# Low, low, high, high: the order of a k-tile's four feature-major products

## The chip, the core and the metric

The kernel runs on one core of one Trainium2 chip. TensorE (PE in the profile) multiplies matrices, VectorE (DVE) and ScalarE (ACT) work element by element, GpSimd (POOL) and SyncE (SP) mostly issue transfers. The metric is the device time of one execution in microseconds (us), taken as the median of several runs.

## The reference

The reference is two transformer-like blocks, one behind the other, on 256 tokens of 2048 features, in float32. The first has two kinds of attention, a gated merge, a feed-forward network and an embedding gate; the second a state-space branch, a gated linear attention, a differential attention, and a feed-forward network with a convolution. Nearly all of the arithmetic is in products of an activation matrix and a large weight matrix, each weight read once:

```
proj = h @ w_in[i]                                   # 2048 x 10240
...
g_ff, u_ff = jnp.split(h @ w_ffn_in[i], 2, axis=-1)  # 2048 x 11264
x = x + (jax.nn.silu(g_ff) * u_ff) @ w_ffn_out[i]
...
proj = hn @ w_in[l]
...
u = h @ w_up                                         # 2048 x 11008
```

## The kernel before

All large products are jobs in one list, and `stream` runs them one after the other. A weight arrives in blocks of 128 x 1024 numbers (512 KB) that SyncE loads; such a block is called a half. To keep nearly all of float32's accuracy, a number is split in two: a high part, rounded to TensorE's one-pass format (`fp32r`), and a low part, the remainder. For weights, ACT makes the high part (line 487, `high`) and DVE the low part (line 497, `low`), a few halves ahead of their use: `CA` = 4 halves for the high part, `SA` = 3 for the low one. Both go to fixed places in one large tile `w`, so a new high or low part waits until TensorE has read the old one in its place. Activations lie as `x = j.acts.at(k)`: 128 features by 512 columns, 256 tokens' high parts and then the same tokens' low parts.

There are two main kinds of job. A token-major job (kind "AS", `mm_as`, lines 591 to 593) has the activations as stationary operand and 512 columns of weights moving; each of its products has 512 columns. A feature-major job (kind "WS", lines 549 to 559) has the weights as stationary operand and the tokens moving. It makes two blocks of 128 output features, f = 0 and f = 1, from 2048 input features, which are 16 k-tiles of 128; one half holds four k-tiles, so a job has four halves. For each k-tile and block there are two products:

- the high product (line 553): high weights times all 512 columns of `x`, into `acc[:, f, :]`
- the low product (line 557): low weights times the 256 high columns of `x`, into `acc[:, f, 256:512]`

The two blocks lie in separate accumulators of 512 numbers each. In the job's first k-tile the high product comes first, since it starts the accumulation (`start=k == first`); in all others the low one does. After the last k-tile the job's evacuation (`ws_sum`: ACT copies one part out at line 445, DVE adds the other at line 446) is put in front of the other waiting work, and the next job begins on the other of two accumulators. Before each new half, the loop issues the splitting of a later half, and after it `self.tick()` lets the rest of the program (attention, norms, evacuations) issue its next piece; small matmuls of that rest so come to stand between two halves. The instructions of each engine are run in the order in which this loop writes them.

Of the kernel before, what the change touches and what calls it, by code (L numbers as in the profile page):

```python
# [188 lines left out]
class Build:  # L189
# [262 lines left out]
    def stream(self, jobs):  # L452
        nc = self.nc
        halves = [(j, i, ks) for j in jobs for i, ks in j.halves]
        N = len(halves)
        raws, spl = {}, {}
        width = lambda j, ks: {"AS": 512 * len(ks), "WS": 1024, "W4": 512}[j.kind]

        W = self.wp.tile([128, (CA + 1) * 1024 + GAP + (SA + 1) * 1024 + WSH], F32R, tag="w", name="w")

        def places(first, bufs):


            far = [False] * (N + 1)
            for i in reversed(range(N)):
                far[i] = halves[i][0].kind == "WS" and (far[i + 1] or i % bufs == bufs - 1)
            at = [first + i % bufs * 1024 + WSH * far[i] for i in range(N)]
            return at, {i for i in range(bufs, N) if far[i] and i % bufs != bufs - 1 and not far[i - bufs + 1]}

        at_h, late_h = places(0, CA + 1)  # L470
        at_l, late_l = places((CA + 1) * 1024 + GAP, SA + 1)

        def load(i):
            j, idx, ks = halves[i]
            n = width(j, ks)
            r = self.rawp.tile([128, 1024], F32, tag="raw", name=self.name("raw"))
            nc.sync.dma_start(out=r[:, :n], in_=self.d[j.w][idx][:, :n])
            raws[i] = r

        def high(i):  # L480
            j, idx, ks = halves[i]
            n = width(j, ks)
            wh = W[:, at_h[i]:at_h[i] + 1024]
            if j.kind == "W4":
                wh = self.ev.tile([128, 512], F32, tag="b", name=self.name("w4"), bufs=1)
            for c in ((0, 512), (512, n)) if i == 0 else ((0, n),):
                nc.scalar.copy(wh[:, c[0]:c[1]], raws[i][:, c[0]:c[1]])  # L487
            spl[i] = wh

        def low(i):  # L490
            j, idx, ks = halves[i]
            n = width(j, ks)
            r, wh = raws.pop(i), spl[i]
            wl = None
            if j.kind != "W4":
                wl = W[:, at_l[i]:at_l[i] + 1024]
                nc.vector.tensor_sub(wl[:, :n], r[:, :n], wh[:, :n].bitcast(F32))  # L497
            spl[i] = (wh, wl)
            if i + RAWB < N:
                load(i + RAWB)  # L500

        ahead = self.at_start(load)

        z = self.ev.tile([128, 512], mybir.dt.bfloat16, tag="b", name="zeros", bufs=1)
        nc.vector.memset(z, 0.0)
        b = self.psp.tile([128, 512], F32, tag="p3", name="idle")
        for _ in range(WARM):
            nc.tensor.matmul(b, lhsT=z[:, 0:128], rhs=z, start=True, stop=True)
        for i in range(CA):
            next(ahead)  # L510
            high(i)
            if i < SA:
                low(i)
        self.add(ahead)
        last, prev, acc = None, None, None
        for i, (j, idx, ks) in enumerate(halves):
            if i + CA < N and i + CA not in late_h:
                high(i + CA)
            if i + SA < N and i + SA not in late_l:
                low(i + SA)  # L520
            if j is not last:
                if j.before is not None:
                    j.before()
                while prev is not None and not prev.free:
                    self.tick(must=True)
                prev, last = last, j
                acc = self.accp.tile([128, 2, 512], F32, tag="acc", name=self.name("acc"))
            for k in ks:
                while k not in j.acts.ready:
                    self.tick(must=True)  # L530
            first, end = j.halves[0][1][0], j.halves[-1][1][-1]
            if j.by_m is not None:

                for m in range(2):
                    for q, (_, _, kq) in enumerate(halves[i:]):
                        self.mm_as(j.acts, kq, *spl[i + q], acc, (m,), first, end)
                    j.by_m(m, acc)
                break
            wh, wl = spl.pop(i)
            if j.kind == "AS":  # L540
                self.mm_as(j.acts, ks, wh, wl, acc, (0, 1), first, end, low_last=i < 2)
            elif j.kind == "W4":

                for k in range(16):
                    p = slice(32 * (k % 4), 32 * (k % 4) + 32)
                    nc.tensor.matmul(acc[p, 0, :], lhsT=wh[:, 32 * k:32 * k + 32],
                                     rhs=j.acts.at(k).bitcast(F32), start=k < 4, stop=k >= 12)
            else:
                for kk, k in enumerate(ks):
                    x = j.acts.at(k)  # L550
                    for f in range(2):
                        s = slice((kk * 2 + f) * 128, (kk * 2 + f) * 128 + 128)
                        hi = lambda: nc.tensor.matmul(  # L553
                            acc[:, f, :], lhsT=wh[:, s], rhs=x, start=k == first, stop=k == end)
                        if k == first:
                            hi()
                        nc.tensor.matmul(acc[:, f, 256:512], lhsT=wl[:, s], rhs=x[:, 0:256], start=False, stop=False)  # L557
                        if k != first:
                            hi()
            if i + CA in late_h:  # L560
                high(i + CA)
            if i + SA in late_l:
                low(i + SA)
            if i + 1 == N or halves[i + 1][0] is not j:
                self.add(j.evac(acc, lambda j=j: setattr(j, "free", True)), front=True)
            self.tick()
        while self.gens:
            self.tick(must=True)
# [1238 lines left out]
```

## Time and profile before

| what | value |
|---|---|
| median of 3 runs | 3137.13 us (3136.98 to 3137.66) |
| the profiled execution, its time | 3137.06 us |
| the profiled execution, its span | 3135.3 us |
| PE busy | 3122.8 us, 17644 matmuls |
| DVE, ACT busy | 1993.8 us, 1551.2 us |
| high products of feature-major jobs (line 553) | 3936 |
| low products of feature-major jobs (line 557) | 3936 |
| token-major products (lines 591, 592, 593) | 2368 each |

The span goes from the first to the last instruction. Matmuls overlap in the records: one of 512 columns is listed with 393 ns, while the next one starts sooner, and their ends are modelled. So the rate is read from the distance of their starts. PEld is the load of a stationary operand; it too overlaps with matmuls.

### The profile page before, as it was taken

How to read it: one execution, taken by the hardware profiler on the slowest of the kernel's cores; microseconds unless marked ns; L12 is line 12 of the kernel's file. 1: busy time of each engine (PE TensorE's matmuls, PEld its weight loads, DVE VectorE, ACT ScalarE, POOL GpSimd, SP SyncE). 2: the span in 40 equal slices, each digit the busy share in tenths (PEclk: the TensorE clock that was granted, in tenths of full speed). 3: DMA queues.
4: the chain of work that ended last, by engine and by line, in shares of the span. 5: the costliest groups of instructions: out<-in, count | busy, mean ns of one | idle time of the engine just before them, and what ended most of it. 6: DMA issues, size and time to landing. Idle time of an engine off the chain costs nothing.

```text
span 3135.3 us, 45198 instructions
## 1 busy us (share of the span) xinstructions
PE 3122.8 (100%) x17644; PEld 2650.9 (85%) x17644; DVE 1993.8 (64%) x2595; ACT 1551.2 (49%) x2035; POOL 73.3 (2%) x158
## 2 busy tenths in 40 slices
PE   9999999999999999999999999999999999999998
PEld 7888888888888888888888888888888888888887
DVE  5656445557577676566655667945555766757766
ACT  6544444455444454456544455444445645545544
POOL 0000000000001000000000001000000000000000
PEclk9999999999999999999999999999999999999999
DMA  7554555555667667655654565655555565565554
GB/s 267 175 179 164 191 192 188 185 186 190 215 226 249 243 229 238 189 175 195 215 178 162 176 219 201 217 183 201 197 187 185 185 196 188 190 198 188 190 188 168
DMA packets 172646, 618.00 MB, mean 197 GB/s; under 512 B 23553, under 2 KB 23969, under 8 KB 169233
## 3 DMA queue, kind: packets, MB, share of 16 engines
q1 hardware_dynamic: 164704, 576.96, 55.9%
q0 software_dynamic: 7440, 37.64, 3.5%
q8 instruction: 138, 2.26, 0.3%
q14 instruction: 76, 0.61, 0.1%
q10 hardware_dynamic: 288, 0.52, 0.0%
HBM read 599.74 MB, written 14.25 MB: 196 GB/s over the span
## 4 chain that ended last, share of the span: by engine, by line
PE 99%; DMA 0%; DVE 0%; ACT 0%; SPq 0%; issue 0%; ACTq 0%
PE acc L553 29%; PE acc L591 17%; PE acc L592 17%; PE acc L593 17%; PE acc L557 15%; PE p L349 1%; PE p L1712 0%; PE p L1752 0%; DMA raw<-in_w_vsb 0%; PE p L1165 0%; PE p L939 0%; PE p L940 0%; PE p L941 0%; PE p L1161 0%; PE p L1755 0%; PE p L1142 0%
## 5 line engine op out<-in xcount | busy, mean ns | idle before, releaser
L497 DVE TENSOR_TENSOR w<-raw,w 128x1024 fp32r<-128x1024 f32 x1088 | 1319.4, 1219 | 642.3 <-PE acc L592 429.1
L487 ACT CAST w<-raw 128x1024 fp32r<-128x1024 f32 (+1 forms) x1089 | 1138.5, 1048 | 1091.8 <-PE acc L593 641.6
L553 PE MATMUL acc<-s,w 128*128 128x512 f32 x3936 | 1369.5, 393 | 0.0
L557 PE MATMUL acc<-s,w 128*128 128x256 f32 x3936 | 1090.4, 282 | 0.0
L591 PE MATMUL acc<-w,s 128*128 128x512 f32 x2368 | 930.5, 393 | 0.8 <-DVE big L1385 0.8
L592 PE MATMUL acc<-w,s 128*128 128x512 f32 x2368 | 922.1, 389 | 0.4 <-DVE w L497 0.4
L593 PE MATMUL acc<-w,s 128*128 128x512 f32 x2368 | 922.0, 389 | 0.0
L553 PEld LDWEIGHTS acc<-s,w 128*128 128x128 f32 x3936 | 733.5, 188 | 153.4
L557 PEld LDWEIGHTS acc<-s,w 128*128 128x128 f32 x3936 | 740.2, 188 | 10.4 <-issue 1.0
L593 PEld LDWEIGHTS acc<-w,s 128*128 128x128 f32 x2368 | 444.5, 188 | 93.6
L591 PEld LDWEIGHTS acc<-w,s 128*128 128x128 f32 x2368 | 444.6, 188 | 93.4 <-issue 1.7
L592 PEld LDWEIGHTS acc<-w,s 128*128 128x128 f32 x2368 | 444.7, 188 | 91.8 <-DVE w L497 1.3
L446 DVE TENSOR_TENSOR s<-acc,s 128x512 f32<-128x512 f32 (+1 forms) x120 | 82.7, 689 | 267.7 <-ACT s L445 267.6
L445 ACT COPY s<-acc 128x512 f32<-128x512 f32 (+1 forms) x120 | 70.1, 584 | 187.4 <-PE acc L553 185.0
L313 ACT ACTIVATE s<-s 128x256 f32<-128x256 f32 (+4 forms) x175 | 76.6, 443 | 106.9 <-DVE s L316 38.1
L316 DVE SCALAR_TENSOR_TENSOR s<-s,conv 128x256 f32<-128x256 f32 x172 | 79.3, 481 | 3.1
L448 DVE TENSOR_TENSOR s<-s,rb 128x512 f32<-128x512 f32 (+1 forms) x104 | 71.7, 689 | 3.5
L321 ACT CAST s<-s 128x256 fp32r<-128x256 f32 (+1 forms) x104 | 45.7, 443 | 29.4 <-DVE s L979 14.3
L1668 DVE TENSOR_TENSOR s<-s,s 128x1024 f32<-128x1024 f32 x48 | 58.4, 1218 | 0.0
L313 ACT ACTIVATE s<-s,conv 128x256 f32<-128x256 f32 x86 | 47.1, 595 | 21.9 <-DVE s L448 21.9
L322 DVE TENSOR_TENSOR s<-s,s 128x256 fp32r<-128x256 f32 (+1 forms) x104 | 47.3, 457 | 15.2 <-ACT s L321 13.9
L313 ACT ACTIVATE junk<-big 128x512 f32<-128x512 f32 x48 | 30.3, 631 | 51.2 <-DVE big L958 32.4
(268 smaller groups left out, 1015.3 us busy)
## 6 DMA issues: line engine op xcount, KB each, us to landing
raw<-in_w_fin SPq DMA_DIRECT2D x176, 512.0 KB, 4.3
raw<-in_w_up SPq DMA_DIRECT2D x172, 512.0 KB, 4.1
raw<-in_w_fout SPq DMA_DIRECT2D x88, 512.0 KB, 4.5
raw<-in_w_down SPq DMA_DIRECT2D x84, 512.0 KB, 4.2
raw<-in_w_qksb SPq DMA_DIRECT2D x32, 512.0 KB, 3.8
raw<-in_w_qkca SPq DMA_DIRECT2D x32, 512.0 KB, 4.2
raw<-in_w_gsb SPq DMA_DIRECT2D x32, 512.0 KB, 4.1
raw<-in_w_gca SPq DMA_DIRECT2D x32, 512.0 KB, 3.8
```

What stands on the lines that cost most here:

```text
L313: self.nc.scalar.activation(out, in_, func, scale=scale, **kw)
L316: self.nc.vector.scalar_tensor_tensor(out=out, in0=in0, scalar=scalar, in1=in1, op0=op0, op1=op1)
L445: nc.scalar.copy(out, acc[:, 0:n, 256:512])
L446: nc.vector.tensor_add(out, acc[:, 0:n, 0:256], out)
L448: nc.vector.tensor_mul(out, out, rb.tile[:, None, :].to_broadcast([128, n, 256]) if n > 1 else rb.tile[:, None, :])
L487: nc.scalar.copy(wh[:, c[0]:c[1]], raws[i][:, c[0]:c[1]])
L497: nc.vector.tensor_sub(wl[:, :n], r[:, :n], wh[:, :n].bitcast(F32))
L553: hi = lambda: nc.tensor.matmul(acc[:, f, :], lhsT=wh[:, s], rhs=x, start=k == first, stop=k == end)
L557: nc.tensor.matmul(acc[:, f, 256:512], lhsT=wl[:, s], rhs=x[:, 0:256], start=False, stop=False)
L591: nc.tensor.matmul(acc[:, m, :], lhsT=xl, rhs=wh[:, s], start=k == first, stop=False)
L592: nc.tensor.matmul(acc[:, m, :], lhsT=xh, rhs=wl[:, s], start=False, stop=False)
L593: nc.tensor.matmul(acc[:, m, :], lhsT=xh, rhs=wh[:, s], start=False, stop=k == end)
```

## The change

In every k-tile of a feature-major job the loop over high and low goes outside the loop over the two blocks. A k-tile other than a job's first ran low f0, high f0, low f1, high f1, and now runs low f0, low f1, high f0, high f1. The first one ran high f0, low f0, high f1, low f1, and now runs high f0, high f1, low f0, low f1. Operands, shapes, places and the order of the additions into each accumulator stay.

```diff
                     x = j.acts.at(k)
-                    for f in range(2):
-                        s = slice((kk * 2 + f) * 128, (kk * 2 + f) * 128 + 128)
-                        hi = lambda: nc.tensor.matmul(
-                            acc[:, f, :], lhsT=wh[:, s], rhs=x, start=k == first, stop=k == end)
-                        if k == first:
-                            hi()
-                        nc.tensor.matmul(acc[:, f, 256:512], lhsT=wl[:, s], rhs=x[:, 0:256], start=False, stop=False)
-                        if k != first:
-                            hi()
+                    for is_low in (False, True) if k == first else (True, False):
+                        for f in range(2):
+                            s = slice((kk * 2 + f) * 128, (kk * 2 + f) * 128 + 128)
+                            if is_low:
+                                nc.tensor.matmul(acc[:, f, 256:512], lhsT=wl[:, s], rhs=x[:, 0:256],
+                                                 start=False, stop=False)
+                            else:
+                                nc.tensor.matmul(acc[:, f, :], lhsT=wh[:, s], rhs=x, start=k == first, stop=k == end)
```

In the changed file the low product is line 555 and the high one line 558. The instructions of DVE, ACT, GpSimd and SyncE keep their order, number and kinds of waits. On TensorE, this is the start of one job, `acc122`, before (s is the tile of the activations, w the weights; like neighbours are one row with x2):

```order
L553 MATMUL acc122_1024<-s40_144,w_105 128x512 [waits PE_49]
L557 MATMUL acc122_1024<-s40_144,w_105 128x256
L553 MATMUL acc122_1024<-s40_144,w_105 128x512
L557 MATMUL acc122_1024<-s40_144,w_105 128x256 x2
L553 MATMUL acc122_1024<-s40_144,w_105 128x512
L557 MATMUL acc122_1024<-s40_144,w_105 128x256
L553 MATMUL acc122_1024<-s40_144,w_105 128x512
L557 MATMUL acc122_1024<-s40_144,w_105 128x256
L553 MATMUL acc122_1024<-s40_144,w_105 128x512
```

The first two highs stand apart, and the only two lows in a row are the last of the first k-tile and the first of the second. The same place on TensorE now:

```order
L558 MATMUL acc122_1024<-s40_144,w_105 128x512 [waits PE_49]
L558 MATMUL acc122_1024<-s40_144,w_105 128x512
L555 MATMUL acc122_1024<-s40_144,w_105 128x256 x4
L558 MATMUL acc122_1024<-s40_144,w_105 128x512 x2
L555 MATMUL acc122_1024<-s40_144,w_105 128x256 x2
L558 MATMUL acc122_1024<-s40_144,w_105 128x512 x2
```

The first k-tile's lows and the second's make a row of four, and from then on lows and highs come in twos. The second place is the seam of two halves of the same job, where small matmuls of an attention (p123) stand between; TensorE before:

```order
L553 MATMUL acc122_1024<-s40_144,w_105 128x512
L721 MATMUL p123_1045<-s119_1011 128x256 [waits DVE_49,PE_49]
L722 MATMUL p123_1045<-s119_1011 128x128
L557 MATMUL acc122_1024<-s43_164,w_105 128x256
L553 MATMUL acc122_1024<-s43_164,w_105 128x512 [waits Activation_49]
L557 MATMUL acc122_1024<-s43_164,w_105 128x256
```

The half's first high, which waits for ACT, is its second product. TensorE now:

```order
L558 MATMUL acc122_1024<-s40_144,w_105 128x512 x2
L720 MATMUL p123_1045<-s119_1011 128x256 [waits DVE_49,PE_49]
L721 MATMUL p123_1045<-s119_1011 128x128
L555 MATMUL acc122_1024<-s43_164,w_105 128x256 x2
L558 MATMUL acc122_1024<-s43_164,w_105 128x512 [waits Activation_49]
L558 MATMUL acc122_1024<-s43_164,w_105 128x512
```

It is now the third product, and the half before ends with two highs, so its last low is read one product earlier.

## Rows read from the trace of the kernel before

**Rows 1.** The page: busy time (share of the span), 40 slices in tenths.

```profile
span 3135.3 us, 45198 instructions
...
PE 3122.8 (100%) x17644; PEld 2650.9 (85%) x17644; DVE 1993.8 (64%) x2595; ACT 1551.2 (49%) x2035; POOL 73.3 (2%) x158
...
PEclk9999999999999999999999999999999999999999
```

**Rows 2.** The page: the chain that ended last, by engine and line.

```profile
PE 99%; DMA 0%; DVE 0%; ACT 0%; SPq 0%; issue 0%; ACTq 0%
...
by line: PE acc L553 28.8%; PE acc L591 17.2%; PE acc L592 17.1%; PE acc L593 17.1%; PE acc L557 14.9%; PE p L349 0.7%; PE p L1712 0.3%; PE p L1752 0.2%; DMA raw<-in_w_vsb 0.2%; PE p L1165 0.2%; PE p L939 0.2%; PE p L940 0.2%; PE p L941 0.2
```

**Rows 3.** PE's waits, all: total us, times, longest us.

```profile
PE idle L508 <- DVE zeros L505: 1.3, 1, 1.3
PE acc L583 <- ACT w L487: 0.8, 2, 0.6
PE acc L591 <- DVE big L1385: 0.8, 1, 0.8
PE acc L592 <- DVE w L497: 0.4, 1, 0.4
```

**Rows 4.** Timeline of PE in token-major work: start us, us, instruction.

```profile
350.12 0.39 PE L591 MATMUL acc<-w,s 128*128 128x512 f32 x1
...
371.88 0.39 PE L591 MATMUL acc<-w,s 128*128 128x512 f32 x1
```

**Rows 5.** Timeline of PE in the middle of a feature-major job.

```profile
2525.36 0.28 PE L557 MATMUL acc<-s,w 128*128 128x256 f32 x1
2525.47 0.39 PE L553 MATMUL acc<-s,w 128*128 128x512 f32 x1
2525.70 0.28 PE L557 MATMUL acc<-s,w 128*128 128x256 f32 x1
...
2533.68 0.28 PE L557 MATMUL acc<-s,w 128*128 128x256 f32 x1
```

**Rows 6.** Timeline of PE at seams of feature-major jobs, the last high first.

```profile
2434.12 0.62 PE L553 MATMUL acc<-s,w 128*128 128x512 f32 x2
...
2523.03 0.62 PE L553 MATMUL acc<-s,w 128*128 128x512 f32 x2
2523.49 0.28 PE L557 MATMUL acc<-s,w 128*128 128x256 f32 x1
2523.61 0.39 PE L553 MATMUL acc<-s,w 128*128 128x512 f32 x1
2523.84 0.40 PE L557 MATMUL acc<-s,w 128*128 128x256 f32 x2
2524.07 0.40 PE L553 MATMUL acc<-s,w 128*128 128x512 f32 x1
2524.31 0.28 PE L557 MATMUL acc<-s,w 128*128 128x256 f32 x1
...
2534.14 0.62 PE L553 MATMUL acc<-s,w 128*128 128x512 f32 x2
```

**Rows 7.** Groups of PE and PEld: count, busy us, mean ns, idle us before.

```profile
L553 PE MATMUL acc<-s,w 128*128 128x512 f32 x3936 | 1369.5, 393 | 0.0
L557 PE MATMUL acc<-s,w 128*128 128x256 f32 x3936 | 1090.4, 282 | 0.0
...
L557 PEld LDWEIGHTS acc<-s,w 128*128 128x128 f32 x3936 | 740.2, 188 | 10.4 <-issue 1.0
```

**Rows 8.** Timeline of PE: a feature-major job behind token-major work, up to its end.

```profile
2809.26 0.39 PE L593 MATMUL acc<-w,s 128*128 128x512 f32 x1
2809.49 0.39 PE L553 MATMUL acc<-s,w 128*128 128x512 f32 x1
...
2820.36 0.62 PE L553 MATMUL acc<-s,w 128*128 128x512 f32 x2
...
2821.16 0.40 PE L557 MATMUL acc<-s,w 128*128 128x256 f32 x2
2821.40 0.40 PE L553 MATMUL acc<-s,w 128*128 128x512 f32 x1
```

**Rows 9.** Waits of the engines that split the weights: total us, times, longest us.

```profile
ACT w L487 <- PE acc L553: 240.5, 187, 3.0
...
DVE w L497 <- PE acc L557: 78.6, 64, 3.8
```

## The prediction

> **What bounds the kernel now.** I read the page from the top. TensorE (PE) is busy for 3122.8 of 3135.3 us, its clock is granted in full (2.4 GHz, the upper of its two levels) in all 40 slices, and the other engines stand at 64% and below [rows 1]. A busy PE alone proves little, since matmuls overlap in the records, so the chain that ended last comes next: 99% of it is PE, and 28.8% and 14.9% of the span are lines 553 and 557, the two lines of the change [rows 2]. Then the list of PE's own waits: in the whole program they are 3.3 us, of which 0.4 us are for a low half of weights from VectorE (DVE) [rows 3]. So nothing feeds PE too late; the time is the rate at which PE starts one matmul after the other. I read that rate from the distances of starts in the timeline, over whole repetitions, since single starts are rounded to 10 ns and the ends are modelled.
>
> Three rates count. In a token-major job every matmul has 512 columns: 96 of them take from 350.12 to 371.88, 226.7 ns each [rows 4]. In the middle of a feature-major job a low (256 columns) and a high (512) alternate: 24 pairs take from 2525.36 to 2533.68, 346.7 ns a pair [rows 5]. If a high costs 226.7 here too, a low costs 120.0; the difference for 256 columns is then 106.7 ns, and twice that for 512 columns is 213.3, so that 13.3 ns remain for each matmul, long or short. Both steady stretches fit "columns plus 13.3 ns", whatever their mix. Last, whole jobs: nine jobs, each of 32 pairs, take from 2434.12 to 2534.14, 11.113 us a job [rows 6]. Thirty-two pairs at 346.7 ns are 11.093. Each job thus loses 0.020 us, and it loses it at the seam, because the middle runs at the steady rate.
>
> **The change, part by part.** The matmuls stay the same in number and shape: 3936 highs and 3936 lows [rows 7], four to a k-tile, so 1968 k-tiles in 123 jobs. The instructions of the other engines stand in the same order as before. What moves is the order inside a k-tile, and with it three things.
>
> *The rate.* In 1845 k-tiles (all but the first of each job) low, high, low, high becomes low, low, high, high. Each k-tile then has one low behind a low and one high behind a high. Before, both neighbourhoods occur at the seam of two jobs alone: the last high of a job stands before the first of the next, and the low that ends the first k-tile stands before the one that begins the second. Their rows: two highs from 2523.03 to 2523.49, 0.46 us, against 0.453 for two at 226.7 ns; two lows from 2523.84 to 2524.07, 0.23 us, against 0.240 [rows 6]. Together 0.69 us, against 0.693 for the k-tile of now. By its four matmuls the new k-tile costs what the old one does. What the seam loses comes just behind the two lows: from the second of them, which starts 0.12 us behind the first, at 2523.96, to the low at 2525.36 four pairs take 1.40 us, where the steady rate gives 1.387 [rows 5, 6]. That row decides the upper bound, because in the new order every two lows are followed not by steady pairs but by the next change of neighbourhood. If each k-tile loses all that a seam loses, 0.020 us, the change costs 1845 x 0.020 = 37 us. From below: the two lows at 0.23 us read up to 0.010 under 2 x 120 ns; since another pair of lows takes 0.24 (2821.16 to 2821.40 [rows 8]), I put it at 0.005 us, and if the highs behind give nothing of it back, that is 1845 x 0.005 = 9 us gained. Between the two ends, a job that follows token-major work has the two lows in its start, but no two highs across its seam: from its first high at 2809.49 to the next job's first high, which begins 0.23 us after the 2820.36 of its row, so at 2820.59, are 11.10 us [rows 8], 0.007 over 32 pairs, with a rounding of 0.010. So two lows alone cost some 5 ns at most, a quarter of the seam. I take 0: two steady stretches of quite different make-up, all long and long with short, both run at 13.3 ns over the columns, and the new order is again a steady repetition, where the seam's loss is that of a change from one pattern to another. Taken: 0 us; ends -9 and +37.
>
> *The seam.* Each job's first k-tile goes high, high, low, low, where it went high, low, high, low, so four highs and then four lows stand in a row. At worst the loss there doubles, at best it goes: 123 x 0.020 = 2.5 us either way; taken 0.
>
> *Due times and releases.* The last reader of a low half now comes one high before the half's end, 0.23 us earlier, so the copy that overwrites it (line 497) may start earlier in each of the 1968 / 4 = 492 halves. DVE waited for these lows 64 times, 78.6 us in all [rows 9]. But what it makes is waited for by PE for 0.4 us in the program [rows 3], so that this is worth 0.4 us at most. The first low of a job comes one high later, the first high of every other half one low (0.12 us) later: slack for DVE and for ScalarE (ACT). The last reader of a high half stays the second block's high, so ACT's 240.5 us of waits for line 553 [rows 9] stay, and so does the start of the evacuation. No DMA and no queue is moved past. Taken 0.
>
> The sum is made against the profiled execution, 3137.06 us, which is 3135.3 of span and 1.8 around it, and 0.07 under the median of the runs, 3137.13: 3137.1 + 0 + 0 + 0 = **3137.1 us**.
>
> A rule of the Trainium skill bears on the two lows: the page "TensorE: Matmul & The Clock Gate", section "LDWEIGHTS (loading the stationary operand)", gives a weight load as its columns over 1.2 GHz, by an estimate from it 107 ns for 128 columns. A low's 115 to 120 ns cover that by some 10 ns, and by the rule alone two lows in a row cost nothing: the sum stays as it is. The records of this kernel give 188 ns for a load [rows 7], more than the distance of two lows, and so speak for the first rival below; but one after another four of them would make 752 ns a k-tile, where 693 pass, so they overlap and set no price.
>
> **The rivals.**
> *Slower: the lows in a row eat a reserve.* PE prepares the next weights and products while the present one runs; behind a high there is twice the time for that as behind a low. If an alternating stream lives on what each high builds up for the low behind it, two lows in a row use it up, and the pairs behind them pay, as the four pairs behind 2523.96 do. For it: a loss at every seam of nine equal jobs, and of equal size. Against it: after token-major work the same two lows cost a quarter of that. It decides against the forecast from 6.3 / 1845 = 3.4 ns a k-tile. At the 5 ns of the start behind token-major work: 1845 x 0.005 = +9, **3146 us**; at the full seam +37, 3174.
> *Faster: lows in a row are cheaper.* If the 0.23 us of two lows holds and the highs run at 226.7, a k-tile takes 0.688 and the program 9 us less: **3128 us**. Against it: the pairs behind the two lows give it all back, and more [rows 6].
> *The change doesn't do what it says* in one sense: if PE's start of a matmul depends on columns alone, no order inside a k-tile shows in the time. That is the forecast itself.
>
> **How the numbers follow.** A measurement of this kernel can tell about 0.2%, 6.3 us, from no change. The forecast, no change that shows (3134.5 to 3143), gets 0.55. The slower rival gets 0.37, of which I put 0.22 under 3151 (a loss of up to 7.5 ns a k-tile: 1845 x 0.0075 = 14 us) and 0.15 above it. The faster one gets 0.08. The range holds the forecast's cases and the cheaper half of the slower ones, 0.77, and a little of the faster: 3134 to 3151. Most of the chance lies on no change and on slower; the forecast's own range is 3134.5 to 3143. So faster 0.08, same 0.55, slower 0.37.
>
> **What would show it.** In the timeline of the changed kernel, twelve k-tiles in the middle of a job should take 8.32 us, as 24 pairs do now, and a job 11.09 to 11.13. If the slower rival is right, the k-tile takes 0.697 us or more throughout the job, two highs behind two lows take over 0.46, and PE still waits for nothing. PE's waits should stay near 3 us, and DVE's for the lows shrink from 78.6. The forecast is wrong if a k-tile's period differs from 0.693 by more than 0.003, for I argue its rate from seams alone, and the trace of before has no steady stretch of the new order.

## The result, and the profile after

The changed kernel takes 3155.54 us (3155.34 to 3155.70 in 4 runs), where the kernel before takes 3137.06 (3136.98 to 3137.66 in 4 runs): 1.0058 times as long, 95% interval 1.0046 to 1.007. It is 18.5 us slower. The forecast, 3137.1 us and no change that shows, was wrong, and the range, 3134 to 3151, does not hold the time.

The page of the changed kernel, against [rows 1, 2]; the high product is now line 558, the low one line 555:

```profile
span 3153.9 us, 45198 instructions
...
PE 3141.6 (100%) x17644; PEld 2654.2 (84%) x17644; DVE 1993.1 (63%) x2595; ACT 1551.7 (49%) x2035; POOL 73.6 (2%) x158
...
PEclk9999999999999999999999999999999999999999
```

PE does the same 17644 matmuls and is busy 18.8 us longer; the clock is granted in full as before, and DVE and ACT are as busy as before. PE's waits, all of them (total us, times, longest us), against [rows 3]:

```profile
PE idle L508 <- DVE zeros L505: 1.3, 1, 1.3
PE acc L590 <- DVE big L1384: 0.8, 1, 0.8
PE acc L582 <- ACT w L487: 0.6, 1, 0.6
PE acc L591 <- DVE w L497: 0.4, 1, 0.4
```

They sum to 3.1 us, where they were 3.3: none has come in. The groups of the two lines (count, busy us, mean ns of one, idle us before), against [rows 7]:

```profile
L558 PE MATMUL acc<-s,w 128*128 128x512 f32 x3936 | 1229.0, 396 | 0.0
...
L555 PE MATMUL acc<-s,w 128*128 128x256 f32 x3936 | 772.7, 283 | 0.0
```

A high is recorded with 396 ns instead of 393, a low with 283 instead of 282. The busy sums of the two lines can't be compared with those of before, since time in which two matmuls overlap is put down to one of them. So the starts have to be read. PE in the middle of a feature-major job (start us, us, instruction; x2 is two alike in one row), against [rows 5]:

```profile
2661.92 0.40 PE L555 MATMUL acc<-s,w 128*128 128x256 f32 x2
2662.16 0.63 PE L558 MATMUL acc<-s,w 128*128 128x512 f32 x2
2662.63 0.40 PE L555 MATMUL acc<-s,w 128*128 128x256 f32 x2
...
2668.99 0.40 PE L555 MATMUL acc<-s,w 128*128 128x256 f32 x2
```

From 2661.92 to 2668.99 ten k-tiles take 7.07 us, 707 ns each, where two pairs of before take 2 x 346.7 = 693.3. Most of the loss sits in the highs. Two lows take 0.24 us (2661.92 to 2662.16) and two highs 0.47 (2662.16 to 2662.63), some 234 ns each. In the middle of a job of before, the next start comes 0.23 us behind a high and 0.11 behind a low [rows 5]; without the timeline's rounding to 10 ns, the trace of before gives 229 and 117.5 ns there, and that of the changed kernel 234 to 235 and 117 to 120. So some 10 of the 13.3 ns are the two highs'. Across two whole jobs, by the four highs in a row at each seam, against [rows 6]:

```profile
2635.39 1.10 PE L558 MATMUL acc<-s,w 128*128 128x512 f32 x4
...
2657.95 1.10 PE L558 MATMUL acc<-s,w 128*128 128x512 f32 x4
```

A job takes 11.28 us, against 11.113: 0.167 more. For 123 jobs that would be 20.5 us, of which 18.5 are measured, because not every job is like these. Compared job by job in the two traces, the 93 jobs without other matmuls inside them lose 0.163 us each, 15.1 in all, and the 30 with small matmuls between their halves 0.110 each, 3.3 in all.

### The profile page after: what moved, and what is told of

It is laid out like the page before. It is cut to its first block, busy times and chain, and to the rows that moved or that the text cites. A ratio compares the mean times of both kernels' runs of the same rounds, so it can differ in the third digit from the quotient of the medians.

```text
span 3153.9 us, 45198 instructions
## 1 busy us (share of the span) xinstructions
PE 3141.6 (100%) x17644; PEld 2654.2 (84%) x17644; DVE 1993.1 (63%) x2595; ACT 1551.7 (49%) x2035; POOL 73.6 (2%) x158
## 3 DMA queue, kind: packets, MB, share of 16 engines
q8 instruction: 138, 2.26, 0.3%
## 4 chain that ended last, share of the span: by engine, by line
PE 99%; DMA 0%; DVE 0%; ACT 0%; SPq 0%; issue 0%; ACTq 0%
PE acc L558 29%; PE acc L590 17%; PE acc L591 17%; PE acc L592 17%; PE acc L555 15%; PE p L349 1%; PE p L1711 0%; DMA raw<-in_w_vsb 0%; PE p L1751 0%; PE p L1164 0%; PE p L938 0%; PE p L939 0%; PE p L940 0%; PE p L1160 0%; PE p L1754 0%; PE p L1141 0%
## 5 line engine op out<-in xcount | busy, mean ns | idle before, releaser
L558 PE MATMUL acc<-s,w 128*128 128x512 f32 x3936 | 1229.0, 396 | 0.0
L555 PEld LDWEIGHTS acc<-s,w 128*128 128x128 f32 x3936 | 724.6, 189 | 165.6 <-issue 1.0
L555 PE MATMUL acc<-s,w 128*128 128x256 f32 x3936 | 772.7, 283 | 0.0
L558 PEld LDWEIGHTS acc<-s,w 128*128 128x128 f32 x3936 | 611.1, 188 | 9.4
```

What stands on the lines that cost most here:

```text
L558: nc.tensor.matmul(acc[:, f, :], lhsT=wh[:, s], rhs=x, start=k == first, stop=k == end)
```

## The experiments

My theory behind the result was that the order of the lengths sets the rate: two products of 512 columns in a row, behind two of 256, run slower. Its rivals: the order in which weights and accumulators are visited; and the prediction's own, a reserve that lows in a row eat up. A further one came up on the way: the place of the weights in SBUF. All rates below are from starts in PE's timeline in the middle of a feature-major job, and the kernel before was run beside each kernel; its median there lay between 3137.2 and 3137.6 us.

**Lengths or places visited: x1_widths_old_order and x2_widths_new_order.** Both give the products of block 0 256 columns, high and low alike, and both of block 1 512 columns, outside a job's first k-tile. So block 0's high weights are not multiplied with the low parts of the tokens, and block 1's low weights are, and the columns stay the same in sum. The old order of operands then has the lengths short, short, long, long, and the new order has them alternate:

```diff
...
+                        c = 0 if f or k == first else 256
+                        nc.tensor.matmul(acc[:, f, c:512], lhsT=wh[:, s], rhs=x[:, 0:512 - c], start=k == first, stop=k == end)
...
+                        c = 0 if f and k != first else 256
+                        nc.tensor.matmul(acc[:, f, c:512], lhsT=wl[:, s], rhs=x[:, 0:512 - c], start=False, stop=False)
```

> The order of the kernel before, low f0, high f0, low f1, high f1, but except in a job's first k-tile both products of block 0 have 256 columns and both of block 1 have 512 (so parts of the products are left out or double: the output is not the reference's). The number of columns is that of before. Lengths now come as short, short, long, long, while weights and accumulators are visited as before. Theory 'lengths' (two short ones in a row cost 13.3 ns a k-tile, as the steady middle of the changed kernel shows): 3155 us, within 3 us. Theory 'places' (what costs is that weights of one kind or other accumulators follow each other): 3137 us, within 3 us.

> The changed kernel's order, low f0, low f1, high f0, high f1, with 256 columns in both products of block 0 and 512 in both of block 1 except in a job's first k-tile (the output is not the reference's). Lengths now alternate short, long, short, long, while weights and accumulators are visited as in the changed kernel. 'Lengths': 3137 us, within 3 us. 'Places': 3155 us, within 3 us.

The old order with the new lengths took 3155.9 us (1.0059, 1.0044 to 1.0074), the new order with the old lengths 3137.37 (1.0001, 0.9991 to 1.001). The first highs of block 0 (256 columns) in the old order, ten k-tiles apart:

```profile
2661.35 0.28 PE L554 MATMUL acc<-s,w 128*128 128x256 f32 x1
...
2668.42 0.28 PE L554 MATMUL acc<-s,w 128*128 128x256 f32 x1
```

and in the new order, where a row joins a short and a long product of the same line:

```profile
2647.31 0.51 PE L554 MATMUL acc<-s,w 128*128 128x256 f32 x2
...
2654.24 0.51 PE L554 MATMUL acc<-s,w 128*128 128x256 f32 x2
```

7.07 against 6.93 us, so 707 and 693 ns a k-tile. With the weights where they lie in these kernels, the loss goes with the order of the lengths. The order in which weights and accumulators are visited is out.

**Which neighbours: lhhl and l4h4.** The first goes low f0, high f0, high f1, low f1, so that the accumulator changes twice in a k-tile; the second takes two k-tiles together, four lows and then four highs:

```diff
...
+                    else:
+                        low_p(kk, k, 0)
+                        high_p(kk, k, 0)
+                        high_p(kk, k, 1)
+                        low_p(kk, k, 1)
```

```diff
...
+                for q in range(0, len(ks), 2):
+                    kf = [(kk, ks[kk], f) for kk in (q, q + 1) for f in range(2)]
+                    for p in (high_p, low_p) if ks[q] == first else (low_p, high_p):
+                        for c in kf:
+                            p(*c)
```

> Low f0, high f0, high f1, low f1 in all k-tiles but a job's first. As a cycle the lengths are those of the changed kernel, short, short, long, long, but the accumulator changes only twice a k-tile, as before, instead of four times. 'Lengths': 3155 us, within 4 us. If the change of the accumulator with every product is what costs: 3137 us, within 4 us.

> Two k-tiles at a time: four lows, then four highs. If every low behind a low (or high behind a high) has its price, there are 1.5 of each a k-tile instead of 1, so the loss of 18 us grows to 28: 3165 us. If the price is paid once for every run of lows, there is half a run a k-tile, the loss halves to 9: 3146 us. If only the change of accumulators counts, it is that of the changed kernel: 3155 us.

lhhl took 3158.57 us (1.0068, 1.0053 to 1.0083), l4h4 3152.38 (1.0048, 1.0033 to 1.0063). Ten k-tiles of lhhl, and four times two k-tiles of l4h4:

```profile
2664.00 0.40 PE L555 MATMUL acc<-s,w 128*128 128x256 f32 x2
...
2671.07 0.40 PE L555 MATMUL acc<-s,w 128*128 128x256 f32 x2
```

```profile
2659.78 0.63 PE L555 MATMUL acc<-s,w 128*128 128x256 f32 x4
...
2665.40 0.63 PE L555 MATMUL acc<-s,w 128*128 128x256 f32 x4
```

lhhl has the 707 ns again; changing the accumulator with every product is not what costs. In l4h4 two k-tiles take 5.62 / 4 = 1.405 us, 18 ns over 2 x 693.3. If each change of length cost something, half as many changes should have halved the loss of 27; if each long behind a long cost something, three of them in place of two should have raised it. It did neither, and lies between what I had written for the two.

**One length alone: x512_all_long and x256_all_short.** The old order, where outside the first k-tile every product has 512 columns (the lows take in the low parts of the tokens too), or 256 (the highs leave them out):

```diff
+                    c = 0 if k == first else 256
...
-                        nc.tensor.matmul(acc[:, f, 256:512], lhsT=wl[:, s], rhs=x[:, 0:256], start=False, stop=False)
+                        nc.tensor.matmul(acc[:, f, c:512], lhsT=wl[:, s], rhs=x[:, 0:512 - c], start=False, stop=False)
...
+                            nc.tensor.matmul(acc[:, f, c:512], lhsT=wh[:, s], rhs=x[:, 0:512 - c], start=False, stop=k == end)
```

with `c = 0` throughout for the long one.

> The order of the kernel before, but every low product has 512 columns too (it adds low weights times low activations, which the reference has and the kernel before leaves out). Read from the middle of a job. If long products behind each other cost nothing of their own, as in token-major work: 226.7 ns each, 453 a pair, and 3137 + 3936 x 0.1067 = 3557 us. If a feature-major long product behind a long one is the dearer thing, as the 234 to 235 ns between the highs of the changed kernel could mean: 234 ns each, 468 a pair, about 3610 us.

> The order of the kernel before, but outside a job's first k-tile every product has 256 columns (high weights times the low part of the activations are left out). Read from the middle of a job: if short products behind each other cost their columns plus 13.3 ns: 120 ns each, 240 a pair, and 3137 - 3690 x 0.1067 = 2743 us. If short ones in a row are held up by something that a long one in between makes good (the reserve): more than 120 ns each; were the whole loss of 13.3 ns a k-tile due to one short one behind another, 133 ns each.

All long took 3572.97 us, in one run, between the 3557 and the 3610 that I had written for the two cases. Its timeline, in which eight small transposes (line 349) stand inside a job:

```profile
2697.27 0.39 PE L558 MATMUL acc<-s,w 128*128 128x512 f32 x1
...
2699.53 0.40 PE L558 MATMUL acc<-s,w 128*128 128x512 f32 x1
2699.77 1.04 PE L349 MATMUL p<-cst,big 128*128 128x128 f32 x8
...
2701.35 0.39 PE L558 MATMUL acc<-s,w 128*128 128x512 f32 x1
...
2711.15 0.39 PE L558 MATMUL acc<-s,w 128*128 128x512 f32 x1
```

Ahead of the transposes ten matmuls take 2.26 us, 226 ns each (226.7, the pace of token-major work, lies within the rounding of the starts); behind them 42 take 9.80, 233.3 each. The same line, the same lengths and the same order of operands run at two paces, and the work in between shifts the stream from one to the other. So a long product behind a long one is not dearer as such, and the pace can hold on until something else comes between.

All short took 2851.48 us, with 42.1 us of waits of PE for DVE's lows in it, so that only its rate counts:

```profile
2428.03 0.28 PE L556 MATMUL acc<-s,w 128*128 128x256 f32 x1
...
2433.01 0.28 PE L556 MATMUL acc<-s,w 128*128 128x256 f32 x1
```

42 matmuls in 4.98 us are 118.6 ns each, within the 120 that the prediction reckoned for a low and 1 ns over the 117.5 behind a low of before. Short products in a row need no reserve at all.

**One pair at a time: llh and lhh.** The changed order without the second high of a k-tile (left out but in the first and the last k-tile), and without the second low (left out but in the first):

```diff
...
+                    else:
+                        low_p(kk, k, 0)
+                        low_p(kk, k, 1)
+                        high_p(kk, k, 0)
+                        if k == end:
+                            high_p(kk, k, 1)
```

```diff
...
+                    else:
+                        low_p(kk, k, 0)
+                        high_p(kk, k, 0)
+                        high_p(kk, k, 1)
```

> The changed kernel's order without the second block's high products, outside a job's first and last k-tile (the second block's main product is left out): low, low, high. It keeps two lows in a row and has no two highs in a row. At columns plus 13.3 ns a k-tile takes 466.7 ns. If the two lows alone make the loss of 13.3 ns: 480.0. If the highs in a row make it: 466.7.

> The changed kernel's order without the second block's low products outside a job's first k-tile (they are left out): low, high, high. It keeps two highs in a row and has no two lows in a row. At columns plus 13.3 ns a k-tile takes 573.3 ns. If the highs in a row make the loss of 13.3 ns: 586.7. If the lows do: 573.3.

llh took 2854.37 us in one run (41.1 us of waits for DVE's lows in it), lhh 2944.68, also in one. Ten k-tiles of llh and eight of lhh:

```profile
2429.33 0.40 PE L555 MATMUL acc<-s,w 128*128 128x256 f32 x2
...
2434.06 0.40 PE L555 MATMUL acc<-s,w 128*128 128x256 f32 x2
```

```profile
2502.61 0.28 PE L555 MATMUL acc<-s,w 128*128 128x256 f32 x1
...
2507.27 0.28 PE L555 MATMUL acc<-s,w 128*128 128x256 f32 x1
```

llh takes 473 ns where 2 x 120 + 226.7 = 466.7 would do, lhh 582 where 120 + 2 x 226.7 = 573.3 would; both lie between the values written for them. With 117.5 and 229 ns, the spacings of before, each still loses, 6 to 9 ns by either split. lhh loses without two lows in a row anywhere in the middle of a job, and all short loses nothing with nothing but lows in a row. The prediction's slower rival falls in its mechanism, and every single pair of neighbours is acquitted in one kernel and accused in another.

**The seam: hlhl.** High, low in every k-tile, the first one too, so that the lengths alternate across the seams of jobs:

```diff
                     for f in range(2):
...
+                        high_p(kk, k, f)
+                        low_p(kk, k, f)
```

> High f0, low f0, high f1, low f1 in every k-tile, the first one too, so that long and short alternate without a break from the first job to the last one (as in the kernel before inside a job, but without its two highs and two lows at the seams). Theory 'alternation' (a break of the one-by-one alternation costs about three highs at 233 instead of 227 ns, 20 ns a seam; the middle of a job has none): jobs of 11.093 us instead of 11.113, at most 123 x 0.020 = 2.5 us less, 3134.7 us. If the seam's loss is due to something else at the change of jobs (a wait, the new accumulator): 3137.2 us, and jobs of 11.113.

It took 3135.58 us (3134.76 to 3135.97 in 11 runs) against 3137.38 (3136.92 to 3137.90 in 15): 0.9993, 0.9984 to 1.0002. The runs of the two don't overlap, but the interval holds 1. Thirty-two pairs, with a seam of two jobs among them:

```profile
2646.27 0.39 PE L551 MATMUL acc<-s,w 128*128 128x512 f32 x1
...
2657.36 0.39 PE L551 MATMUL acc<-s,w 128*128 128x512 f32 x1
```

They take 11.09 us, where a job of before takes 11.113 [rows 6]: the seam's 20 ns go when the alternation is not broken. 123 x 0.020 is 2.5 us, and 1.8 were measured. It is the fastest of the kernels that leave no product out, by less than one can be sure of.

**The place of the weights.** High and low weights of feature-major work, but for a few halves at the end of a stretch, lie 4 numbers (16 bytes) further on in the tile `w` than those of token-major work: `WSH = 4`. The next kernels change this constant alone, 0, 2, 6 and 8 in the changed order, 0 and 8 in the old one. It is also part of the length of `w`, but the activations lie ahead of `w` and stay in place:

```diff
-WSH = 4
+WSH = 0
```

> The changed kernel, with all weights of feature-major jobs at places 4 numbers (16 bytes) lower (the kernel keeps them 4 numbers off a multiple of 1024 by a constant, WSH). Theory 'addresses' (a weight load and the moving operand's read run at the same time, and hold each other up depending on where both lie and on how far apart in time they are; the order of lengths sets the latter): the k-tile's 706.7 ns change with the shift, to 693.3 or to still more. Theory 'lengths alone' (the order of lengths makes the loss, wherever the operands lie): 706.7 ns, 3155 us.

> The changed kernel with WSH 8 in place of 4, the weights of feature-major jobs 16 bytes higher. As for the run with WSH 0: 'addresses' expects another k-tile than 706.7 ns in at least one of the two, 'lengths alone' 706.7 ns and 3155 us in both.

> The kernel before with WSH 0. 'Addresses': the pair's 346.7 ns change, if the shift was what kept this order free of the loss: up to 353 ns a pair (a high at 233 instead of 227), 3137 + 3936 x 0.0067 = 3163 us. 'Lengths alone': 346.7 ns and 3137 us.

> The changed kernel with WSH 2 (8 bytes below its place now, 8 above that of WSH 0). If the loss depends on steps of 16 bytes or more alone: the 696.7 ns of WSH 0 or the 706.7 of WSH 4. If finer: another value. If the new order costs nothing by itself, some shift should come near 693.3 ns a k-tile and 3137 us.

> The changed kernel with WSH 6. As for WSH 2: the 706.7 ns of WSH 4 or the 702 of WSH 8 if only steps of 16 bytes count; a value of its own if finer ones do; near 693.3 if this is a place without loss.

> The kernel before with WSH 8. If its 346.7 ns a pair are the luck of one place: over 346.7, as with WSH 0 (352.1), 3145 to 3163 us. If WSH 0 is the exception: 346.7 and 3137 us.

One run each, the two known kernels beside them, with the time of a k-tile in the middle of a job:

| shift of the weights | old order | new order |
|---|---|---|
| 0 | 3154.41 us, 707 ns | 3142.34 us, 697 ns |
| 2 | not run | 3143.82 us, 699 ns |
| 4 (as the kernels stand) | 3137 us, 693 ns | 3155.5 us, 707 ns |
| 6 | not run | 3156.66 us, 706.5 ns |
| 8 | 3144.06 us, 693 to 707 ns, by job | 3152.01 us, 703 ns |

Ten k-tiles of the new order at 0, and twenty pairs of the old order at 0:

```profile
2651.48 0.40 PE L555 MATMUL acc<-s,w 128*128 128x256 f32 x2
...
2658.45 0.40 PE L555 MATMUL acc<-s,w 128*128 128x256 f32 x2
```

```profile
2659.86 0.28 PE L557 MATMUL acc<-s,w 128*128 128x256 f32 x1
...
2666.93 0.28 PE L557 MATMUL acc<-s,w 128*128 128x256 f32 x1
```

6.97 us are 697 ns a k-tile, 7.07 us are 353.5 ns a pair. Sixteen bytes slow the old order nearly as much as the change does (3154.4 against 3155.5 us), and win back nearly three quarters of what the new one loses. So neither loss belongs to the order alone.

At 8 the old order runs at either pace, and not by job alone. Inside one job of before_w8 two tiny matmuls (line 1528) part the two:

```profile
734.56 0.28 PE L557 MATMUL acc<-s,w 128*128 128x256 f32 x1
...
738.80 0.28 PE L557 MATMUL acc<-s,w 128*128 128x256 f32 x1
...
739.16 0.28 PE L1528 MATMUL p<-lam,cst 128*128 128x2 f32 x2
...
739.73 0.28 PE L557 MATMUL acc<-s,w 128*128 128x256 f32 x1
...
741.81 0.28 PE L557 MATMUL acc<-s,w 128*128 128x256 f32 x1
```

Twelve pairs ahead of them take 4.24 us, 353.3 ns each, and six behind them 2.08, 346.7 each. As in x512_all_long, what ran before counts beside order and place.

**The lows' place alone: after_g60, then after_l0 and before_l0.** `GAP` sets the distance behind the high weights at which the low ones begin. At 60 in place of 64 all lows come to lie 16 bytes lower, those of token-major work too:

```diff
-GAP = 64
+GAP = 60
```

> The changed kernel with the low weights 16 bytes lower (GAP 60 in place of 64) and the high ones where they are. If the place of each weight against the activations counts: the loads of the lows stand as with WSH 0, those of the highs as with WSH 4, and a k-tile takes something between 696.7 and 706.7. If the lows' place against the highs' counts: any change, also above 706.7; by that the uniform shifts of WSH would have changed nothing, and they did.

It took 3159.32 us in one run, and I had missed both halves of why. Feature-major work, ten k-tiles, and token-major work, 96 matmuls as in [rows 4]:

```profile
2665.73 0.40 PE L555 MATMUL acc<-s,w 128*128 128x256 f32 x2
...
2672.66 0.40 PE L555 MATMUL acc<-s,w 128*128 128x256 f32 x2
```

```profile
349.89 0.39 PE L592 MATMUL acc<-w,s 128*128 128x512 f32 x1
...
371.86 0.39 PE L592 MATMUL acc<-w,s 128*128 128x512 f32 x1
```

6.93 us: the new order runs at 693 ns a k-tile, without any loss. And 21.97 / 96 = 228.9 ns, where it was 226.7: token-major work, which the change doesn't touch, has become slower with the place of its moving operand, the low weights. In the trace the loss stands behind line 591, the product that reads them: 233 ns to the next start where it was 227, while lines 590 and 592 keep 227. The last two kernels keep the first and leave out the second: only the lows of feature-major jobs lie 16 bytes lower, in the changed order and in the old one.

```diff
-        def places(first, bufs):
+        def places(first, bufs, shift):
...
-            at = [first + i % bufs * 1024 + WSH * far[i] for i in range(N)]
+            at = [first + i % bufs * 1024 + shift * far[i] for i in range(N)]
...
-        at_h, late_h = places(0, CA + 1)
-        at_l, late_l = places((CA + 1) * 1024 + GAP, SA + 1)
+        at_h, late_h = places(0, CA + 1, WSH)
+        at_l, late_l = places((CA + 1) * 1024 + GAP, SA + 1, 0)
```

> The changed kernel with the low weights of feature-major jobs 16 bytes lower (their shift 0 in place of 4), those of token-major jobs and all high ones where they are. Theory 'order and place together': 693.4 ns a k-tile in the middle of a job as with GAP 60, token-major work at 227.0 ns, and 3155.5 - 1845 x 0.0133 = 3131 us at best; with the loss at the seams that the kernel before has too, 3137 us within 4. If the new order costs by itself and GAP 60 saved it in another way: 3155 us.

> The kernel before with the same place of the lows. 'Order and place together': the place that suits the new order need not suit the old one; anything between 346.7 and 353 ns a pair, 3137 to 3163 us. If this place is simply better for every order: 3137 us or a little less.

The changed order took 3136.97 us (3136.75 to 3137.38 in 10 runs; 0.9999, 0.9989 to 1.0008), the old one 3153.03 (3152.81 to 3153.45 in 4 runs; 1.0049, 1.0033 to 1.0066). Ten k-tiles and a job of the changed order, then twenty pairs of the old one:

```profile
2643.57 1.10 PE L558 MATMUL acc<-s,w 128*128 128x512 f32 x4
...
2647.52 0.40 PE L555 MATMUL acc<-s,w 128*128 128x256 f32 x2
...
2654.45 0.40 PE L555 MATMUL acc<-s,w 128*128 128x256 f32 x2
2654.69 1.10 PE L558 MATMUL acc<-s,w 128*128 128x512 f32 x4
```

```profile
2659.97 0.28 PE L557 MATMUL acc<-s,w 128*128 128x256 f32 x1
...
2667.04 0.28 PE L557 MATMUL acc<-s,w 128*128 128x256 f32 x1
```

6.93 us and 11.12 a job against 7.07 us. Set side by side, the median times of the kernels before and after, and of these two, with the highs shifted by 4 numbers in all four, are:

| | lows at 4 | lows at 0 |
|---|---|---|
| low, high, low, high | 3137.1 us | 3153.0 us |
| low, low, high, high | 3155.5 us | 3137.0 us |

Either edit alone costs 16 to 18 us, and both together cost nothing. The effect is neither of the order nor of the place, but of the two together.

## Why the prediction was wrong

- **The rate**, taken at 0 with ends of -9 and +37 us: this step failed. The steady k-tile costs 13.3 ns more, and over the 1845 k-tiles the measured 18.5 us are 10.0 ns each on average. The step of the argument that fell is "two steady stretches of quite different make-up, all long and long with short, both run at 13.3 ns over the columns, and the new order is again a steady repetition". Both stretches ran at that rate because their operands lie where this costs nothing; x512_all_long shows a steady repetition at 233.3 ns, before_w0 and before_l0 show the very order of before at 353.5 ns a pair in place of 346.7, and after_g60 shows token-major work at 228.9. "Columns plus 13.3 ns" is no law of the single product either. It rests on "if a high costs 226.7 here too", and in the trace of before a high in this stream takes 229 ns and a low 117.5; only their sum, 346.7, was measured.
- **What was known of it.** The forecast named the gap itself: the trace of before has no steady stretch of the new order. The 20 ns of a seam, which I set aside as the price of a change of pattern, was the only row that showed the new neighbourhoods, and the value found lies between it and the 5 ns behind token-major work. Where the one row that shows the new pattern shows a loss, a value of 0 by analogy was the wrong choice between the ends. The rows of the seam were also too coarse for the decision: two highs at 0.46 and two lows at 0.23 gave "0.69 us, against 0.693", but unrounded the trace has 0.462 and 0.235, 0.697 in all, 3.7 ns over the old k-tile, where the prediction's point of decision was 3.4.
- **The slower rival** had the sign, and its sizes of 3146 and 3174 us enclose the result; its point of decision, 3.4 ns a k-tile, was passed. Its mechanism was wrong. x256_all_short runs lows alone at 118.6 ns, and lhh loses 6 to 9 ns a k-tile without two lows in a row. The lost time is recorded in the highs, as it had said ("two highs behind two lows take over 0.46": they take 0.47), but after_l0, with the same lows in a row and no loss, shows that this is no repayment of what lows used up.
- **The faster rival** was mis-summed, without effect on the forecast: two lows at 0.23 us and two highs at 226.7 ns are 0.683 us a k-tile and 18 us gained; its 0.688 and 9 us take half of that.
- **The seam**, taken at 0 within 2.5 us, was off too, the other way. Fifteen k-tiles at 13.3 ns more would be 0.200 us a job, and 0.167 was measured, so the start of a job gives back 0.033 of the loss, 4.1 us over 123 such jobs. At a place without the loss (after_l0) the term is 0: a job takes 11.12 us with four highs and four lows in a row at its start, within the rounding of the 11.113 of before. That the seam of before costs 20 ns because the alternation breaks there is borne out by hlhl.
- **Due times and releases**, taken at 0, held. DVE's waits for the lows and ACT's for the highs, against [rows 9], with ACT's for the last line of token-major work, first now and then before:

```profile
ACT w L487 <- PE acc L592: 627.5, 397, 3.5
ACT w L487 <- PE acc L558: 255.4, 221, 3.0
...
DVE w L497 <- PE acc L555: 72.1, 62, 3.5
```

```profile
ACT w L487 <- PE acc L593: 641.6, 407, 3.5
```

DVE waits 6.5 us less for the lows. ACT waits 14.9 us more for the highs, which the prediction had staying, but 14.1 less for token-major work, so no more in sum. PE waits 1.0 us for the two in the whole program (0.6 and 0.4, above). The bound itself (PE's rate, not its supply) was read rightly.
- **The rule on weight loads** that I weighed could not tell: with the same loads of the same size, a k-tile takes 693 or 707 ns by their place.

What stays open is the mechanism under it. The runs show that the time between two matmuls depends on the addresses of the weights and, at the same addresses, on the lengths and on what ran before. That fits a load of weights and the read of a moving operand which get in each other's way when both come at the same time to some of the same parts of SBUF: lengths and earlier work shift the one against the other in time, addresses decide whether they meet. But no run moved the activations or separated load from matmul, so this is argued, not shown. The Trainium skill speaks against it: the page "TensorE: Matmul & The Clock Gate", section "Step-by-step: what each phase is for", says of PE's two read ports that "Loading the next tile's weights doesn't steal SBUF read bandwidth from the running matmul." Here the place of the low weights alone moves a k-tile between 693 and 707 ns and the program by 16 to 18 us, in a stream where PE waits for no other engine. On the effect the measurement decides; on the cause both remain open. The traffic of the other engines is an unlikely cause: over the fifth to fifteenth k-tiles of the changed kernel's 93 uninterrupted jobs, those in which VectorE is idle take 706.1 ns and those in which it is busy nearly throughout 706.5.

## What to carry to other kernels

In a stream that PE alone bounds, the order of long and short products and the place of the weights, down to 16 bytes, are one knob: whoever reorders products should try the placement again before judging the order, and whoever moves a tile should look at the rates of all that reads it. Read such rates as the time of ten or more whole repetitions, since 13 ns in 693 don't show in the mean of a group (393 against 396 ns) and yet are 0.6% of the program. A small loss at the one place where the old kernel already does what the new one will always do is a price to take, not an exception to explain away.

## What the runs showed of the hardware that I had not expected

- The spacing of products of 512 columns in a stream without waits, at the full clock, is not one number: 226.7 ns, 228.9, 229, 233.3 and some 234 were seen, by place, order and what ran before. For alternating pairs it is 346.7 or 353.5 ns.
- The pace can last: in x512_all_long the stream runs at 226 ns ahead of eight transposes and at 233.3 for the 42 matmuls that were counted behind them, with the same order and shift; in before_w8 two tiny matmuls stand between 353.3 ns a pair and 346.7.
- A shift of 8 bytes, between shifts of 4 and 2 numbers, is enough to move the new order from 707 to 699 ns a k-tile.
- Moving the low weights by 16 bytes slowed a product that reads them as its moving operand (226.7 to 228.9 ns), so that one tile's place serves two kinds of job with different best values.
